# Low parts of the attention weights on GpSimd (POOL) in a two-block network

## The chip, the cores and the metric

The kernel runs on one core of a Trainium2 chip. The metric is the device time of one execution in microseconds. Engines are called by the names of the profile: PE is TensorE, PEld its weight load, DVE is VectorE, ACT is ScalarE, POOL is GpSimd, SP issues most transfers.

## The reference, cut to what matters

The reference is two transformer-like blocks on 256 tokens of width 1024, in float32. The part that the change touches is the token mixer of the first block:

```python
z_hy, q, k, v, gates = jnp.split(h @ w_in, SPLITS, axis=-1)
y_hy = hyena_branch(z_hy, conv_w, conv_b, filt, hy_bias) @ w_hy_out
q, k = apply_axial_rope(q, *rope), apply_axial_rope(k, *rope)
k = jnp.concatenate([k, ctx_kv[0]], axis=1)      # 256 more keys from the context
v = jnp.concatenate([v, ctx_kv[1]], axis=1)
...
p = jax.nn.softmax(s, axis=-1)
p = p[:, :, 0] - lam * p[:, :, 1]                # two softmax maps a head
```

Eight heads of 2 x 64 attend from 256 queries to 512 keys. Before the mixer stands a feed-forward network for tokens and context, after it a second one, then the second block with a recurrent branch, banded attention and sixteen experts.

## The kernel before

**Products in two parts.** TensorE multiplies rounded float32 numbers. To keep the precision, each operand is written as a high part, which is the rounded number, and a low part, which is the rest, and each product is three matmuls: high x high, high x low and low x high (`mm3`). `split` makes the two parts: ACT copies the source to the high part and DVE subtracts the high part from the source.

**Weights.** `weights` loads one block of 1024 x 256 weights (tile raw) through SP's queue and splits it in four pieces of 128x512, so each block costs four copies on ACT (whi) and four subtractions (wlo, line 140). There are three buffers for raw and two for each of the parts: the parts of a block can only be written when the matmuls of the block two before it are through.

**The attention groups.** `mixer` first ends the Hyena branch (`hyena_conv`, lines 734 to 736 multiply spectra on DVE) and then runs four groups of two heads. `kvq` makes one group's keys, queries and values from three weight blocks: the key block (512 columns of tokens and context), the query block, the value block. Keys and queries get a rotary embedding in `rope`: four DVE instructions that write tiles rb and ra (lines 765 to 768), then a split (kl, ql). Woven between these steps run the steps of `attend` for the group before: scores, exponentials on ACT, the scaling and sum of the two softmax maps on DVE (p, lines 958 to 961), transposes on TensorE (line 964), the split of the transposed map (pTl), the product with the values.

**Order.** The program text gives each instruction a priority. At the build a planner walks the whole program and writes a fixed order for each engine, taking the first in priority among the instructions that it believes to be ready. On the chip each engine then runs its list strictly in order and waits at semaphores. POOL has little in its list in this stage: the issue of the rotary table's transfer (line 821).

Of the kernel before, what the change touches and what calls it, by code (L numbers as in the profile page):

```python
# [20 lines left out]
T = 256  # L21
# [47 lines left out]
class Net:  # L69
# [52 lines left out]
        self.wp = self.pool(f"wp{n_raw}{n_split}", 1, side="left", es=self.wes)  # L122


    def weights(self, src, ring=False):

        nc = self.nc
        kt, cols = src.shape[1:]
        raw = self.raw_tile() if ring else self.wp.tile([128, kt, cols], F32, name="raw", tag="raw", bufs=self.n_raw)
        nc.sync.dma_start(out=raw, in_=src)  # L130
        hi = self.wp.tile([128, kt, cols], F32R, name="whi", tag="whi", bufs=self.n_split)
        lo = self.wp.tile([128, kt, cols], F32R, name="wlo", tag="wlo", bufs=self.n_split)
        n = max(1, min(kt, CUT // cols))
        for k in range(0, kt, n):
            self.split(raw[:, k:k + n], hi[:, k:k + n], lo[:, k:k + n])
        return hi, lo

    def split(self, src, hi, lo, eng=None):
# [11 lines left out]
        for _ in self.gemm_steps(*args, **kw):  # L150
            pass

    def gemm_steps(self, src, x, n, consume, c0=0, c1=None, steps=1, ring=False, whole=False):


        i = 0
        for c in range(c0, src.shape[0] if c1 is None else c1):
            hi, lo = self.weights(src[c], ring)
            kt, w = src.shape[2:]
            for m in range(w // 128):  # L160
                ps = self.mm([128, n])
                s = slice(m * 128, m * 128 + 128)
                for k in range(kt):
                    with self.tc.high_priority() if whole and k % (kt // steps) else ExitStack():
                        self.mm3(ps, (hi[:, k, s], lo[:, k, s]), (x[0][:, k, :], x[1][:, k, :]), k == 0, k == kt - 1)
                    if k < kt - 1 and (k + 1) % (kt // steps) == 0:
                        yield
                consume(i, ps)
                i += 1
                yield  # L170
# [290 lines left out]
    def first_ffn(self):  # L461
# [21 lines left out]
        with ExitStack() as es2:  # L483
# [13 lines left out]
            def weights(n):  # L497
# [3 lines left out]
                for i in range(2):  # L501
                    self.split(w[i][0][:, s], w[i][1][:, s], w[i][2][:, s])

            weights(0)
            diag = []
            for i in range(4):
# [16 lines left out]
            for f in range(KT + 1):  # L523
                if f < KT:
                    if f + 1 < KT:
                        raws.append(self.ada_load(f + 1, tmp))
                        if f % 2:
                            weights(f // 2 + 1)
                    row = self.ada_rows_of(raws[f], tmp)
                    ps = self.aux([128, 2 * T])  # L530
                    self.turned(ps, x, f, diag)
                if f:
                    products(f - 1, (0, 1))
                if f < KT:
                    a = self.ada_columns(f, row)
                    for i in range(2):
                        t = self.wk.tile([128, T], F32, name="nt", tag="nt", bufs=3)
                        nc.scalar.activation(out=t, in_=ps[:, cut[i]], func=AF.Identity, scale=a[:, i:i + 1],
                                             bias=self.mods[:, f, i:i + 1])
                        self.split(t, h[0][:, f, cut[i]], h[1][:, f, cut[i]])  # L540
                if f:
                    products(f - 1, (2, 3))
# [243 lines left out]
    def mixer(self):  # L786
        nc = self.nc
        w = self.A["w_in"]
        h = self.h
        hx = [x[:, :, 0:T] for x in h]  # L790
        with ExitStack() as es:
# [32 lines left out]
            values = lambda: [pa.tile([128, 4, 256], F32R, name=f"v{q}", tag=f"v{q}", bufs=2) for q in "hl"]  # L824

            def kvq(g, kk, qq, v):
                hi, lo = self.weights(w[16 + g])
                for m in range(2):
                    ps = self.mm([128, 2 * T])
                    s = slice(m * 128, m * 128 + 128)  # L830
                    for k in range(KT):
                        self.mm3(ps, (hi[:, k, s], lo[:, k, s]), (h[0][:, k, :], h[1][:, k, :]), k == 0, k == KT - 1)
                        if k == 3:
                            yield
                    t = [pa.tile([128, 2 * T], F32R, name=f"k{q}", tag=f"k{q}", bufs=3) for q in "hl"]
                    self.rope(pa, ps[:, 0:T], rope[:, 2:4, :], t[0][:, 0:T], t[1][:, 0:T])
                    self.split(ps[:, T:], t[0][:, T:], t[1][:, T:])
                    kk.append(t)
                    yield

                def q_done(m, ps):
                    t = [pa.tile([128, T], F32R, name=f"q{q}", tag=f"q{q}", bufs=3) for q in "hl"]
                    self.rope(pa, ps, rope[:, 0:2, :], t[0], t[1])
                    qq.append(t)

                yield from self.gemm_steps(w, hx, T, q_done, 12 + g, 13 + g)
                hi, lo = self.weights(w[20 + g])
                v += values()
                for tt in range(4):
                    ps = self.mm([128, 256])  # L850
                    s = slice(tt * 128, tt * 128 + 128)
                    for k in range(KT):
                        self.mm3(ps, (h[0][:, k, s], h[1][:, k, s]), (hi[:, k, :], lo[:, k, :]), k == 0, k == KT - 1)
                    self.split(ps, v[0][:, tt, :], v[1][:, tt, :])
                    yield

            side = iter(())
            for g in range(4):
                kk, qq, v = [], [], []
                self.weave(kvq(g, kk, qq, v), side)  # L860
                for _ in side:
                    pass
                side = self.attend(pa, qq, kk, v, g, o)
            gate = [x.bitcast(F32)[:, m, :] for x in values() for m in range(4)]
            for _ in range(2):
                for q in "hl":
                    x = pa.tile([128, 2 * T], F32, name="gda", tag=f"k{q}", bufs=3)
# [1109 lines left out]
```

## Time and profile before

| | |
|---|---|
| median of 3 runs | 1811.67 us (1810.1 to 1814.51) |
| the profiled execution | 1813.05 us |
| its span, first to last instruction | 1811.3 us |
| PE busy | 1687.9 us (93%) |
| DVE busy | 1009.7 us (56%) |
| ACT busy | 706.9 us (39%) |
| POOL busy | 19.9 us (1%) |
| mean granted clock of PE | 0.925 |

The busy times come from one profiled execution. PE's matmuls are pipelined and their ends are modelled, so its share is not the share of its peak. The attention groups take the stretch from about 505 to 700 us; the last quarter of the span is bound by the loads of the experts' weights.

### The profile page before, as it was taken

How to read it: one execution, taken by the hardware profiler on the slowest of the kernel's cores; microseconds unless marked ns; L12 is line 12 of the kernel's file. 1: busy time of each engine (PE TensorE's matmuls, PEld its weight loads, DVE VectorE, ACT ScalarE, POOL GpSimd, SP SyncE). 2: the span in 40 equal slices, each digit the busy share in tenths (PEclk: the TensorE clock that was granted, in tenths of full speed). 3: DMA queues.
4: the chain of work that ended last, by engine and by line, in shares of the span. 5: the costliest groups of instructions: out<-in, count | busy, mean ns of one | idle time of the engine just before them, and what ended most of it. 6: DMA issues, size and time to landing. Idle time of an engine off the chain costs nothing.

```text
span 1811.3 us, 33886 instructions
## 1 busy us (share of the span) xinstructions
PE 1687.9 (93%) x13847; PEld 1275.4 (70%) x13847; DVE 1009.7 (56%) x2502; ACT 706.9 (39%) x1515; POOL 19.9 (1%) x41
## 2 busy tenths in 40 slices
PE   8999999999999999999999999999999878787776
PEld 5788787788998889999999798888874222222222
DVE  3888776768987776676665768877740000000001
ACT  3532223657545568456444653456640000000001
POOL 0000000000000000000000000000010000000000
PEclk9999999999999999999999899999999676767678
DMA  8666673423432214546543331112799999999997
GB/s 330 217 219 231 220 260 112 133 82 121 155 108 94 91 70 140 187 148 248 187 163 117 115 123 61 49 61 76 298 400 400 409 408 409 409 408 409 408 409 303
DMA packets 97768, 397.85 MB, mean 220 GB/s; under 512 B 11227, under 2 KB 13708, under 8 KB 84044
## 3 DMA queue, kind: packets, MB, share of 16 engines
q1 hardware_dynamic: 91728, 386.97, 56.9%
q10 hardware_dynamic: 3724, 4.77, 0.8%
q0 software_dynamic: 2160, 3.94, 0.8%
q8 instruction: 109, 1.79, 0.4%
q14 instruction: 47, 0.39, 0.1%
HBM read 394.59 MB, written 1.05 MB: 218 GB/s over the span
## 4 chain that ended last, share of the span: by engine, by line
PE 68%; DMA 19%; DVE 8%; ACT 3%; issue 1%; DVEq 0%; ACTq 0%; SPq 0%
PE mm L145 13%; PE mm L147 12%; PE mm L146 12%; DMA raw<-exp_w_down 7%; DMA raw<-exp_w_gate 7%; PE mm L1572 4%; PE a L1383 4%; PE at L145 4%; PE at L146 4%; PE at L147 4%; PE a L1740 3%; DMA araw<-w_adat 2%; DMA raw<-exp_w_up 2%; DVE wlo L140 2%; DVE ajunk L310 2%
## 5 line engine op out<-in xcount | busy, mean ns | idle before, releaser
L139 ACT CAST whi<-raw 128x512 fp32r<-128x512 f32 x542 | 309.4, 618 | 260.6 <-PE mm L146 133.1
L140 DVE TENSOR_TENSOR wlo<-raw,whi 128x512 fp32r<-128x512 f32 x542 | 356.5, 686 | 97.8 <-ACT whi L139 93.5
L145 PE MATMUL mm<-hh,whi 128*128 128x256 f32 (+1 forms) x784 | 245.8, 315 | 0.5 <-DVE kl L140 0.5
L147 PE MATMUL mm<-hh,wlo 128*128 128x256 f32 (+1 forms) x784 | 244.9, 314 | 0.5 <-DVE wlo L140 0.2
L146 PE MATMUL mm<-hl,whi 128*128 128x256 f32 (+1 forms) x784 | 244.0, 312 | 0.0
L1707 DVE TENSOR_SCALAR scat<-iota,col 128x256 f32<-128x256 f32 x16 | 6.5, 412 | 275.0 <-PE a L1740 275.0
L145 PEld LDWEIGHTS mm<-hh,whi 128*128 128x128 f32 x784 | 147.2, 188 | 13.2 <-issue 3.5
L146 PEld LDWEIGHTS mm<-hl,whi 128*128 128x128 f32 x784 | 147.3, 188 | 9.9 <-issue 0.8
L147 PEld LDWEIGHTS mm<-hh,wlo 128*128 128x128 f32 x784 | 146.9, 188 | 10.0 <-DVE wlo L140 1.1
L1572 PE MATMUL mm<-raw,ehid 128*32 128x256 f32 x960 | 100.1, 513 | 40.6 <-DMA raw<-exp_w_down 40.2
L1744 ACT COPY ys<-mm 128x256 f32<-128x256 f32 (+1 forms) x20 | 7.2, 362 | 303.4 <-PE mm L1572 293.2
L310 DVE SCALAR_TENSOR_TENSOR ajunk<-araw,scr 128x512 bf16<-128x512 f32 x160 | 110.2, 689 | 27.6 <-DMA araw<-w_adat 25.5
L1572 PE MATMUL mm<-raw,xg 128*32 128x256 f32 x1024 | 103.1, 489 | 20.4 <-DMA raw<-exp_w_gate 20.4
L145 PE MATMUL at<-hh,whi 128*128 128x512 f32 (+1 forms) x352 | 118.7, 337 | 0.0
L147 PE MATMUL at<-hh,wlo 128*128 128x512 f32 (+1 forms) x352 | 118.4, 336 | 0.0
L146 PE MATMUL at<-hl,whi 128*128 128x512 f32 (+1 forms) x352 | 118.1, 336 | 0.0
L145 PE MATMUL mm<-whi,hidh 128*128 128x512 f32 x264 | 105.5, 400 | 1.1 <-ACT hidh L139 0.6
L147 PE MATMUL mm<-whi,hidl 128*128 128x512 f32 x264 | 104.8, 398 | 0.5 <-DVE hidl L140 0.4
L146 PE MATMUL mm<-wlo,hidh 128*128 128x512 f32 x264 | 104.8, 397 | 0.0
L1572 PEld LDWEIGHTS mm<-raw,ehid 128*32 128x32 f32 x960 | 23.7, 123 | 113.7 <-DMA raw<-exp_w_down 95.5
L1572 PE MATMUL a<-raw,xg 128*32 128x256 f32 x1024 | 83.9, 482 | 8.8 <-DMA raw<-exp_w_up 8.8
L145 PE MATMUL mm<-h2h,whi 128*128 128x256 f32 x296 | 89.7, 304 | 0.0
(630 smaller groups left out, 3391.9 us busy)
## 6 DMA issues: line engine op xcount, KB each, us to landing
raw<-exp_w_gate SPq DMA_DIRECT2D x128, 512.0 KB, 10.2
raw<-exp_w_up SPq DMA_DIRECT2D x128, 512.0 KB, 10.2
raw<-exp_w_down SPq DMA_DIRECT2D x120, 512.0 KB, 10.2
raw<-w_ff_in SPq DMA_DIRECT2D x42, 1024.0 KB, 4.8
raw<-w_in SPq DMA_DIRECT2D x32, 1024.0 KB, 4.7
araw<-w_adat SPq DMA_DIRECT2D x56, 512.0 KB, 4.7
raw<-w_ff_out SPq DMA_DIRECT2D x20, 1024.0 KB, 4.9
raw<-w_fill SPq DMA_DIRECT2D x22, 512.0 KB, 3.5
```

The source lines that it names most:

```text
L139: self.high = self.nc.scalar.copy(out=hi, in_=src)
L140: self.low = (eng or self.nc.vector).tensor_tensor(out=lo, in0=src, in1=hi.bitcast(F32), op=ALU.subtract)
L145: nc.tensor.matmul(out=ps, lhsT=w[0], rhs=x[0], start=first, stop=False)
L146: nc.tensor.matmul(out=ps, lhsT=w[0], rhs=x[1], start=False, stop=False)
L147: nc.tensor.matmul(out=ps, lhsT=w[1], rhs=x[0], start=False, stop=last)
L310: nc.vector.scalar_tensor_tensor(out=junk, in0=raw[:, s], scalar=1.0, in1=self.scr[v][:, s], op0=ALU.mult, op1=ALU.mult, accum_out=part[:, ...
L1383: self.nc.tensor.matmul(out=ps[r], lhsT=w[r], rhs=x[r], start=start, stop=stop)
L1572: nc.tensor.matmul(out=ps[q], lhsT=x(k), rhs=raw[:, j, :], start=(k == 0), stop=(k == KT - 1))
L1707: nc.vector.tensor_scalar(out=sc, in0=self.iota[:, 0:T], scalar1=col[:, 0, e:e + 1], scalar2=col[:, 1, e:e + 1], op0=ALU.is_equal, op1=ALU ...
L1740: nc.tensor.matmul(out=acc(tt, j), lhsT=sc[q, tt * 128:tt * 128 + 128], rhs=ys[q], start=False, stop=False)
L1744: nc.scalar.copy(out=ys, in_=ps)
```

## The change

The low parts of the twelve weight blocks that `kvq` loads (key, query and value of four groups) are subtracted by POOL in place of DVE. The operation and its operands are the same. All other blocks, and all other splits, stay on ACT and DVE. `split` had the argument for the engine already.

```diff
-    def weights(self, src, ring=False):
+    def weights(self, src, ring=False, low=None):
...
-            self.split(raw[:, k:k + n], hi[:, k:k + n], lo[:, k:k + n])
+            self.split(raw[:, k:k + n], hi[:, k:k + n], lo[:, k:k + n], low)
...
-    def gemm_steps(self, src, x, n, consume, c0=0, c1=None, steps=1, ring=False, whole=False):
+    def gemm_steps(self, src, x, n, consume, c0=0, c1=None, steps=1, ring=False, whole=False, low=None):
...
-            hi, lo = self.weights(src[c], ring)
+            hi, lo = self.weights(src[c], ring, low)
...
             def kvq(g, kk, qq, v):
-                hi, lo = self.weights(w[16 + g])
+                hi, lo = self.weights(w[16 + g], low=nc.gpsimd)
...
-                yield from self.gemm_steps(w, hx, T, q_done, 12 + g, 13 + g)
-                hi, lo = self.weights(w[20 + g])
+                yield from self.gemm_steps(w, hx, T, q_done, 12 + g, 13 + g, low=nc.gpsimd)
+                hi, lo = self.weights(w[20 + g], low=nc.gpsimd)
```

## Rows read from the trace of the kernel before

**Rows 1.** The page, chain that ended last: share of the span by engine

```profile
PE 68%; DMA 19%; DVE 8%; ACT 3%; issue 1%; DVEq 0%; ACTq 0%; SPq 0%
```

**Rows 2.** Busy time by stretch: start:end, length, engines, granted clock, DMA

```profile
505.00:528.00 23.00, 23.00 (x131) 19.52 (x130) 17.98 (x35) 7.60 (x14) 0.00 (x0) 1.00 0.26 92
...
585.00:626.00 41.00, 40.10 (x275) 34.37 (x274) 31.12 (x74) 23.02 (x51) 0.00 (x0) 1.00 0.22 78
```

**Rows 3.** Waits of PE, 505 to 668 us: total us, times, longest

```profile
PE at L964 <- DVE p L961: 2.3, 7, 0.5
PE mm L145 <- DVE kl L140: 0.5, 1, 0.5
```

**Rows 4.** Groups by line on DVE, 500.0 to 650.1 us: busy, mean ns | idle

```profile
L140 DVE TENSOR_TENSOR wlo<-raw,whi 128x512 fp32r<-128x512 f32 x48 | 32.0, 685 | 4.4 <-ACT whi L139 4.1
```

**Rows 5.** Groups by line on POOL, whole span

```profile
L140 POOL TENSOR_TENSOR hm<-hf,hm 128x256 fp32r<-128x256 f32 x8 | 6.0, 780 | 4.3 <-ACT hm L139 4.3
L1403 POOL COPY ip<-r 128x128 f32<-128x128 f32 x8 | 2.2, 297 | 645.3 <-DMA r<-r 512.8 <-PE a L1383 132.5
```

**Rows 6.** Timeline of DVE and POOL, 1336 to 1345 us: start, duration

```profile
1336.77 0.48 DVE L1625 TENSOR_SCALAR hf<-sx,rr 128x512 f32<-128x512 f32 x1
1336.86 0.98 POOL L140 TENSOR_TENSOR hm<-hf,hm 128x256 fp32r<-128x256 f32 x1 [4.34 <-ACT hm L139]
1337.16 0.96 DVE L1625 TENSOR_SCALAR hf<-sx,rr 128x512 f32<-128x512 f32 x1
...
1340.04 0.72 POOL L140 TENSOR_TENSOR hm<-hf,hm 128x256 fp32r<-128x256 f32 x1
1340.35 0.55 DVE L1647 TENSOR_TENSOR sel<-top,slotmask 16x128 f32<-16x128 f32 x1
...
1344.29 0.26 DVE L1647 TENSOR_TENSOR sel<-top,slotmask 16x128 f32<-16x128 f32 x1
```

**Rows 7.** Timeline of ACT and PE, first group's value weight

```profile
528.22 2.19 ACT L139 CAST whi<-raw 128x512 fp32r<-128x512 f32 x4 [6.67 <-PE mm L146]
...
534.46 0.28 PE L145 MATMUL mm<-whi,hh 128*128 128x256 f32 x1
```

**Rows 8.** Timeline of ACT and DVE, third group, 600 to 605 us

```profile
600.74 1.66 ACT L139 CAST whi<-raw 128x512 fp32r<-128x512 f32 x3 [0.24 <-PE mm L146]
...
601.89 0.42 DVE L767 TENSOR_TENSOR rb<-rb,rope 128x256 f32<-128x256 f32 x1
602.22 0.75 DVE L961 SCALAR_TENSOR_TENSOR p<-p,st 128x512 f32<-128x512 f32 x1
...
603.55 0.68 DVE L140 TENSOR_TENSOR wlo<-raw,whi 128x512 fp32r<-128x512 f32 x1
604.15 0.42 DVE L140 TENSOR_TENSOR kl<-ra,kh 128x256 fp32r<-128x256 f32 x1
604.49 0.68 DVE L140 TENSOR_TENSOR pTl<-at,pTh 128x512 fp32r<-128x512 f32 x1
```

**Rows 9.** Timeline of PE, the same stretch

```profile
603.11 0.30 PE L964 MATMUL at<-ident,p 128*128 128x128 f32 x1 [0.18 <-DVE p L961]
...
605.44 0.28 PE L146 MATMUL at<-pTl,vh 128*128 128x256 f32 x1
```

**Rows 10.** Timeline of ACT, DVE and PE, third group, 609 to 617 us

```profile
609.49 2.18 ACT L139 CAST whi<-raw 128x512 fp32r<-128x512 f32 x4 [1.42 <-PE mm L146]
...
615.75 0.74 DVE L961 SCALAR_TENSOR_TENSOR p<-p,st 128x512 f32<-128x512 f32 x1
...
616.54 0.33 PE L964 MATMUL at<-ident,p 128*128 128x128 f32 x1
```

**Rows 11.** Hyena products: groups on DVE, 500.0 to 650.1 us; timeline of PE

```profile
L736 DVE TENSOR_TENSOR prod<-prod 128x512 f32<-128x512 f32 x4 | 2.8, 690 | 0.1
...
511.97 0.38 PE L145 MATMUL at<-dft2h,yah 128*128 128x256 f32 x1
```

**Rows 12.** Waits of SP's queue, 1180 to 1340 us

```profile
SPq L130 <- DVE wlo L140: 78.1, 9, 14.4
```

## Prediction

> **What bounds the kernel now.** I read the page first. In the chain of work that ended last TensorE holds 68% and DMA 19% of the span, DVE 8% [rows 1]: most of the kernel is a queue of matmuls, and what DVE or POOL do counts only where TensorE waits for it. So the next view is the busy time by stretch [rows 2]. The changed weights are split between 500 and 650 us, and there TensorE is busy 23.00 of 23 us beside the last Hyena products and 40.10 of 41 us in a whole attention group, at a granted clock of 1.00, while DVE is busy 31.12 of 41 us and POOL not at all. The reader is to see that TensorE is full and DVE three quarters full: DVE's load is no bound as such. The list of TensorE's waits says what is left to win [rows 3]: 2.3 us for the scaled softmax rows p (seven times) and 0.5 us for a key's low part. Last I walked the timeline of one group, because the loss, if there is one, lies in the order of a few instructions on DVE.
>
> **What the change takes away.** Twelve weights (key, query and value in four groups) of four pieces make 48 low parts of 128x512, 32.0 us of DVE at 685 ns [rows 4]. TensorE does not run on DVE's load, so all that this can give back is the waits of [rows 3], some 3 us.
>
> **What it adds: 48 subtractions on POOL.** The same instruction runs on POOL in this kernel at half the size: 128x256, eight times, 780 ns mean [rows 5], 0.72 us when undisturbed [rows 6]. Twice that is 1.44 us, the upper bound for 128x512. For the lower bound I take the whole 297 ns of the 128x128 copy [rows 5] as a part that does not grow, and get 0.30 + 2 x (0.72 - 0.30) = 1.14 us. I take 1.25 us from one start to the next, since starts of neighbours lie closer than their durations. The Trainium skill, "GPSIMD Engine Reference", section "Performance versus the Vector engine", gives 4497 ns for 2048 elements; a quarter of it, 1.12 us, is an estimate from that page, and no run here shows it. By it the sum below would be some 2 us less.
>
> Is POOL in time? The tightest weight is the first group's value weight: its high parts start at 528.22 us and TensorE wants it from 534.46 us [rows 7]. The first high part is there at 528.84, so four low parts are there at 528.84 + 4 x 1.25 = 533.8. TensorE takes the last quarter only after 18 matmuls of 0.12 us, at 536.6, so POOL would be late only above (536.6 - 528.84) / 4 = 1.9 us a piece. Waiting for POOL itself costs nothing.
>
> **What it does to DVE.** [Rows 6] show DVE and POOL in each other's way. A DVE multiplication of 128x512 takes 0.48 us at 1336.77; the next one, issued while POOL subtracts from 1336.86 on, takes 0.96 us. The product sel of two SBUF tiles takes 0.26 us with POOL idle at 1344.29, and 0.55 us at 1340.35, where POOL's subtraction lasts from 1340.04 to 1340.76: it waited until POOL was nearly through. POOL's own first piece, begun during DVE's multiplication, took 0.98 in place of 0.72 us. So the two take turns by whole instructions. That they would not, or that larger DVE instructions escape, is the first rival. The Trainium skill says it more widely, "SBUF — State Buffer", section "SBUF: two separate sides": DVE with two SBUF inputs or in a two-port mode and GpSimd share one pair of ports under an exclusive lock, held for the whole instruction. The trace agrees with the 0.55 against 0.26 us; with the full 1.44 us as the time of the lock the sum below would be about 4 us more. This rule speaks against the change.
>
> Now the walk through one group, with 1.25 us a piece [rows 8, 9]. POOL's first piece can start when the first of the high parts is done, 600.74 + 0.62 = 601.4, and ends at 602.65. DVE's rotary product rb (two SBUF inputs) comes at 601.89, waits until 602.65 and ends at 602.98. POOL's second piece stands ready and takes 602.98 to 604.23. The scaled sum p, issued at 602.22 before, waits for it and ends at 604.98, 2.0 us later than before. TensorE's transposes of p wait 0.18 us for it already at 603.11 [rows 9], so they come 2.0 us later. It goes on: POOL 604.98 to 606.2, ra after it until 606.5, kl from the PSUM side until 606.8, POOL's fourth piece until 607.75, the second kl until 608.1, and pTl starts at 608.1 in place of 604.49. Its product stands at 605.44 on TensorE, so TensorE loses another 1.6 us. The one low part that DVE no longer does in this stretch (603.55) is counted in that. Sum: 3.6 us for the stretch, and three groups have it: 10.8 us.
>
> The next key weight falls on the same group's second half [rows 10]: high parts from 609.49 us, POOL from 610.1 to about 616. The products before p and p itself wait up to four times 1.25 us, while four low parts (4 x 0.65 = 2.6 us) leave DVE ahead of p; the rest, 5.0 - 2.6 = 2.4 us at most and nothing at least, I take at 1.2 us. TensorE takes p without a pause at 616.54, so it has no slack. Two groups: 2.4 us.
>
> In the first group there is no softmax yet. POOL's four pieces of the query weight (507.6 to about 513.7) fall among the Hyena products of two SBUF tiles, 0.69 us each [rows 11]. Two of them and one sum stand ahead of the matmul at 511.97 us; with the two low parts of DVE gone from there (1.3 us) and three waits of up to 1.25 us it comes 2.5 us later. The value weight then meets the two rotary steps of the keys, four products and two kl of two SBUF inputs. TensorE waits for the first kl already [rows 3]; at one wait of 1.25 us for each of POOL's four pieces less the 1.2 us of two low parts this is 3.8 us. Sum of the first group: 6.3 us, at least nothing where TensorE has other work.
>
> All together 10.8 + 2.4 + 6.3 = 19.5 us if every engine keeps its order. It will not: the order is made anew at the build with a lighter DVE, which can put p and pTl ahead of some waits. Lower bound for the effect of this: only the first wait of each of the three stretches is left, 3 x 2.0 = 6 us. Between 6 and 19.5 I take 15, nearer to the walk, since the rows of TensorE are full and each order leaves DVE's chain behind it. Later stages pass it on: the last loads wait for buffers that the split frees (78.1 us in nine waits [rows 12]), so the expert weights start later by as much.
>
> **The rivals.** First, DVE's waits are hidden, because the new order keeps the shared products out of POOL's time: then 0 to -3 us is left, 1811 us, no change. For it: DVE idles 10 of 41 us. Against it: TensorE has no slack at the chains. Second, the other side: DVE is relieved of 32 us, p and kl come sooner, and the new order also closes gaps beside the waits; the waits are worth 3 us, and it decides only if the order gains as much again, 1806 us. Against it: TensorE is busy 40.10 of 41 us. Third, POOL becomes the bound: if a piece with DVE's turns between takes more than 1.9 us, value weights come late; at 2.6 us that is 4 x 0.7 = 2.8 us in each of four groups, 11 us on top of the 15, 1838 us. Against it: 0.98 us was the longest at half size, 1.96 at double.
>
> **The numbers.** The profiled execution took 1813.05 us (span 1811.3), 1.4 us above the median of 1811.67; the 15 us are added to the median: 1827 us. Its own range is 1818 to 1832. Chances: the forecast 0.62, hidden 0.20, relief 0.05, POOL as bound 0.13. About 0.3% (5.4 us) is what this measurement can tell from no change. Slower holds the first and the last: 0.75; no change 0.20; faster 0.05. The range takes in most of the hidden case (1811) and reaches to the third rival: 1810 to 1838.
>
> **What the profile after would show.** The row of wlo on POOL, 48 times at 1.2 to 1.45 us; DVE's p, rb and ra with longer means than 0.75 and 0.42 us; the waits of TensorE for p, pTl and kl at over 10 us in place of 2.8; no wait of TensorE for a low part on POOL; and all stages after 700 us moved by the same amount. I am wrong if DVE's two-input products keep their durations beside POOL, or if they stretch and TensorE's waits stay near 3 us.

## The result, and the profile after

The changed kernel takes 1836.39 us (median of 4 runs, 1834.50 to 1840.87) against 1813.09 us before (median of 4, 1810.10 to 1816.13). The ratio is 1.0127 with a 95% interval of 1.0104 to 1.0150: slower by 23 us. The forecast was 1827 us, slower, in a range of 1810 to 1838. The profiled execution took 1834.5 us (span 1832.7).

Where does the time come in? Up to the mixer's Hyena products both traces run level. From 505 us on the one after falls behind step by step, is 23.4 us late at a matmul behind the third group's last scores (673.1 us before, 696.5 after), and some 20 to 23 us late from there to the end. So the loss is made in the stretch of the mixer in which the changed weights are split, and is passed on. The chain of work that ended last names the engines [rows 1]:

```profile
PE 65%; DMA 22%; DVE 9%; ACT 3%; issue 1%; DVEq 0%; SPq 0%; ACTq 0%
```

That says little: 23 of 1836 us are too few for shares. The useful view is the busy time of one stretch in which all kernels of this study do the same matmuls (two of them with some extra ones): from the first transposed Hyena input (uth on ACT) to the first matmul of the Hyena output weight. Columns as in [rows 2]. Before:

```profile
463.21:738.86 275.65, 271.45 (x1978) 245.40 (x1977) 209.02 (x456) 161.55 (x325) 0.53 (x1) 1.00 0.31 106
```

After:

```profile
462.53:762.26 299.73, 280.69 (x1978) 254.31 (x1976) 208.43 (x408) 161.17 (x325) 66.11 (x49) 0.97 0.29 97
```

The stretch is 24.1 us longer, and this splits in two. TensorE's idle time goes from 275.65 - 271.45 = 4.20 to 299.73 - 280.69 = 19.04 us: 14.8 us more. Its busy time, with the same 1978 matmuls, goes from 271.45 to 280.69: 9.2 us more, and the granted clock of the stretch is 0.97 in place of 1.00.

**The idle time.** The list of TensorE's waits, 505 to 692 us after, answers [rows 3]:

```profile
PE at L964 <- DVE p L961: 13.1, 8, 4.0
PE at L145 <- ACT yah L139: 3.0, 1, 3.0
PE at L145 <- ACT pTh L139: 1.6, 2, 0.8
PE aux L1211 <- DVE orms L979: 0.4, 2, 0.2
```

The waits for p grew from 2.3 to 13.1 us. The wait for a key's low part is gone, and no line names a low part of a weight: POOL is in time. Its row, same stretch (groups by line):

```profile
L140 POOL TENSOR_TENSOR wlo<-raw,whi 128x512 fp32r<-128x512 f32 x48 | 65.6, 1396 | 152.8 <-ACT whi L139 152.8
```

The groups by line on DVE, 462.53 to 762.26 us after:

```profile
L961 DVE SCALAR_TENSOR_TENSOR p<-p,st 128x512 f32<-128x512 f32 x16 | 14.0, 873 | 0.3
L768 DVE TENSOR_TENSOR ra<-ra,rb 128x256 f32<-128x256 f32 x16 | 12.9, 806 | 0.2
L767 DVE TENSOR_TENSOR rb<-rb,rope 128x256 f32<-128x256 f32 x16 | 11.8, 739 | 0.0
...
L960 DVE TENSOR_SCALAR p<-p,st 128x512 f32<-128x512 f32 x16 | 8.4, 527 | 0.0
...
L140 DVE TENSOR_TENSOR kl<-ra,kh 128x256 fp32r<-128x256 f32 x8 | 6.8, 847 | 0.9 <-ACT kh L139 0.3
L140 DVE TENSOR_TENSOR vl<-mm,vh 128x256 fp32r<-128x256 f32 x16 | 6.6, 420 | 9.7 <-ACT vh L139 9.7
...
L140 DVE TENSOR_TENSOR kl<-mm,kh 128x256 fp32r<-128x256 f32 x8 | 3.3, 415 | 0.0
```

The same groups before, 463.21 to 738.86 us:

```profile
L961 DVE SCALAR_TENSOR_TENSOR p<-p,st 128x512 f32<-128x512 f32 x16 | 12.0, 748 | 0.3
...
L768 DVE TENSOR_TENSOR ra<-ra,rb 128x256 f32<-128x256 f32 x16 | 6.7, 419 | 0.0
L767 DVE TENSOR_TENSOR rb<-rb,rope 128x256 f32<-128x256 f32 x16 | 6.7, 416 | 0.0
```

The reader is to compare the two kinds of kl: the one that subtracts two SBUF tiles (kl from ra) takes 847 ns, the one with a PSUM input (kl from mm) 415, and so does vl. The instructions of DVE that got longer read two SBUF tiles, with one exception, the scaling of p on line 960, which reads one tile and a column (480 ns before, 527 after). DVE's busy time is about that of before (208.43 and 209.02 us) although 48 instructions left it.

One wait in full: the timeline of DVE at the second group's value weight. POOL's four pieces run from 564.01 to 569.36.

```profile
563.65 0.42 DVE L767 TENSOR_TENSOR rb<-rb,rope 128x256 f32<-128x256 f32 x1
563.98 0.16 DVE L958 RECIPROCAL st<-st 128x2 f32<-128x2 f32 x1
564.10 1.49 DVE L768 TENSOR_TENSOR ra<-ra,rb 128x256 f32<-128x256 f32 x1
565.52 1.24 DVE L959 TENSOR_TENSOR st<-st,nlam 128x1 f32<-128x1 f32 x1
566.68 0.41 DVE L140 TENSOR_TENSOR kl<-mm,kh 128x256 fp32r<-128x256 f32 x1
567.01 1.23 DVE L960 TENSOR_SCALAR p<-p,st 128x512 f32<-128x512 f32 x1
568.17 1.48 DVE L140 TENSOR_TENSOR kl<-ra,kh 128x256 fp32r<-128x256 f32 x1
569.57 0.74 DVE L961 SCALAR_TENSOR_TENSOR p<-p,st 128x512 f32<-128x512 f32 x1
```

Four instructions stand for most of a piece of POOL each, with one that has a PSUM input (kl from mm, 0.41) between them: ra 1.49 in place of 0.42, the factor of one column 1.24 in place of 0.16, the scaling of p 1.23 in place of 0.48, kl 1.48 in place of 0.42. Then POOL is done, and p itself takes its normal 0.74. On TensorE, whose transposes wait for it:

```profile
570.46 0.63 PE L964 MATMUL at<-ident,p 128*128 128x128 f32 x4 [4.00 <-DVE p L961]
```

The third group answers [rows 8, 9]. DVE:

```profile
611.75 1.18 DVE L767 TENSOR_TENSOR rb<-rb,rope 128x256 f32<-128x256 f32 x1
612.85 1.75 DVE L961 SCALAR_TENSOR_TENSOR p<-p,st 128x512 f32<-128x512 f32 x1
614.52 1.49 DVE L768 TENSOR_TENSOR ra<-ra,rb 128x256 f32<-128x256 f32 x1
...
616.49 0.94 DVE L140 TENSOR_TENSOR kl<-ra,kh 128x256 fp32r<-128x256 f32 x1
617.35 0.68 DVE L140 TENSOR_TENSOR pTl<-at,pTh 128x512 fp32r<-128x512 f32 x1
```

TensorE:

```profile
614.75 0.63 PE L964 MATMUL at<-ident,p 128*128 128x128 f32 x4 [1.95 <-DVE p L961]
...
616.99 0.58 PE L145 MATMUL at<-pTh,vh 128*128 128x256 f32 x1 [0.79 <-ACT pTh L139]
```

The second of these waits comes by way of ACT, which makes the key's high part kh from the late ra before it makes pTh:

```profile
616.05 0.41 ACT L139 CAST kh<-ra 128x256 fp32r<-128x256 f32 x1 [2.95 <-DVE ra L768]
616.36 0.58 ACT L139 CAST pTh<-at 128x512 fp32r<-128x512 f32 x1
```

**The longer matmuls.** Busy time by stretch, just behind the 4.00 us wait:

```profile
570.50:571.80 1.30, 1.30 (x11) 1.13 (x11) 1.27 (x5) 0.59 (x1) 0.00 (x0) 1.00 0.48 88
571.80:575.20 3.40, 3.40 (x16) 3.40 (x17) 0.97 (x2) 0.41 (x1) 0.00 (x0) 0.50 0.59 248
575.20:578.00 2.80, 2.75 (x19) 2.07 (x18) 1.67 (x4) 2.12 (x5) 1.05 (x1) 1.00 0.00 0
```

From 571.8 us TensorE has work without a break but is granted 0.50, its 1.2 GHz level, and gets 16 matmuls done in 3.4 us, 0.21 us each against 0.12 just before. The records of the clock show this at five places, 20.5 us in all: from 513.8, 571.8, 616.2 (6.8 us), 633.2 and 667.4 us, each at the end of a wait of 1.95 us or more or within 1.5 us behind it, but for the last, which follows two waits of 1.95 and 0.79 us close together. Before, the clock was 1.00 in the whole stretch. Not all of the 9.2 us need be the clock: the kernel with quarter pieces (below) is 2.0 us more busy than before with no lower clock at all.

### The profile page after: what moved, and what is told of

Read it like the earlier page. It is cut to its first block, busy times and chain, and to the rows that moved or that the text cites. A ratio compares the mean times of both kernels' runs of the same rounds, so it can differ in the third digit from the quotient of the medians.

```text
span 1832.7 us, 33891 instructions
## 1 busy us (share of the span) xinstructions
PE 1675.5 (91%) x13847; PEld 1267.0 (69%) x13847; DVE 1009.4 (55%) x2454; ACT 706.3 (39%) x1515; POOL 86.0 (5%) x89
## 4 chain that ended last, share of the span: by engine, by line
PE 65%; DMA 22%; DVE 9%; ACT 3%; issue 1%; DVEq 0%; SPq 0%; ACTq 0%
PE mm L145 13%; PE mm L147 13%; PE mm L146 13%; DMA raw<-exp_w_down 7%; DMA raw<-exp_w_up 6%; DMA raw<-exp_w_gate 6%; PE a L1383 4%; PE at L145 4%; PE at L146 4%; PE at L147 3%; DMA araw<-w_adat 2%; PE mm L1572 2%; DVE ajunk L310 2%; DVE wlo L140 1%; PE a L1740 1%
## 5 line engine op out<-in xcount | busy, mean ns | idle before, releaser
L140 DVE TENSOR_TENSOR wlo<-raw,whi 128x512 fp32r<-128x512 f32 x494 | 324.6, 686 | 91.2 <-ACT whi L139 88.1
L147 PEld LDWEIGHTS mm<-hh,wlo 128*128 128x128 f32 x784 | 148.4, 190 | 10.2 <-DVE wlo L140 1.2
L1572 PE MATMUL mm<-raw,xg 128*32 128x256 f32 x1024 | 99.4, 483 | 8.4 <-DMA raw<-exp_w_gate 8.1
L1718 DVE TENSOR_TENSOR ea<-ea,a 128x256 f32<-128x256 f32 x16 | 6.7, 421 | 159.5 <-PE a L1572 159.5
## 6 DMA issues: line engine op xcount, KB each, us to landing
raw<-exp_w_gate SPq DMA_DIRECT2D x128, 512.0 KB, 10.2
raw<-exp_w_up SPq DMA_DIRECT2D x128, 512.0 KB, 10.2
raw<-exp_w_down SPq DMA_DIRECT2D x120, 512.0 KB, 10.2
```

Source lines behind the costliest of these rows:

```text
L140: self.low = (eng or self.nc.vector).tensor_tensor(out=lo, in0=src, in1=hi.bitcast(F32), op=ALU.subtract)
L147: nc.tensor.matmul(out=ps, lhsT=w[1], rhs=x[0], start=False, stop=last)
L1572: nc.tensor.matmul(out=ps[q], lhsT=x(k), rhs=raw[:, j, :], start=(k == 0), stop=(k == KT - 1))
L1718: nc.vector.tensor_tensor(out=a, in0=a, in1=u, op=ALU.mult)
```

## The experiments

Three theories. **A**, that of the prediction with the clock added: DVE's instructions on two SBUF tiles and POOL's take turns by whole instructions, TensorE waits for the chain behind them, and long waits let its clock fall. **B**: the lighter DVE list gets another order at the build, and that order costs the time. **C**: POOL's low parts are late (four take 5.5 us in place of 2.7), and what needs them or their buffers is late. Edits are shown against the kernel after. Every kernel was timed beside the one before, whose median was 1810.6 to 1812.0 us in these series. Rows are of the stretch defined above, from one profiled execution of each kernel. The growth of this stretch comes within 2 us of the growth of the median in all kernels but two: with p in PSUM it is 14.1 us against 18.8, in the first fill 28.3 against 24.5.

### Adding alone, removing alone

```diff
-            self.split(raw[:, k:k + n], hi[:, k:k + n], lo[:, k:k + n], low)
+            self.split(raw[:, k:k + n], hi[:, k:k + n], lo[:, k:k + n]); low and low.tensor_tensor(out=self.spare, ...)
```

> DVE keeps all 48 low parts, and POOL does the same 48 subtractions once more into a tile that nobody reads. Theory A (DVE instructions with two SBUF inputs and POOL's take turns; the waits let TensorE's clock fall): nothing is taken off DVE and POOL is in the way as often, so the loss is at least that of the change, 20 to 32 us: 1833 to 1845 us, TensorE's idle time of 510 to 697 us at 15 us or more in place of 3.25, and low granted clocks behind the long waits. Theory B (the lighter DVE list and the new order that follows from it cost the time): DVE's list is as long as before, so no loss, 1813 us. Theory C (POOL's low part is late, 5.5 us a weight in place of 2.7, and what waits for it or for its buffers is late): nobody reads POOL's tile, so 1813 to 1816 us.

Measured: 1849.25 us, ratio 1.0214 (1.0196 to 1.0233), 38 us slower, more than the change itself.

```profile
461.63:776.40 314.77, 287.16 (x1978) 259.12 (x1977) 250.89 (x456) 161.78 (x325) 73.52 (x49) 0.94 0.26 93
```

Idle time is 27.61 us, 23.4 more than before, busy time 15.7 us more, with 37.5 us at the lower clock. B in its form (a lighter list) and C fall as sole causes: DVE has all its 456 instructions, and nobody reads what POOL writes. DVE's order still differs from that before in some twenty places, so what a new order costs is left to the next kernel. The size lies above my 20 to 32 us: DVE's own low parts wait too (902 ns mean in place of 685), and TensorE now waits for them:

```profile
PE mm L146 <- DVE wlo L140: 2.0, 2, 1.3
```

The opposite:

```diff
-        lo = self.wp.tile(..., name="wlo", ...)
+        lo = self.wp.tile(..., name="wlo", ...) if not low else hi
-            self.split(raw[:, k:k + n], hi[:, k:k + n], lo[:, k:k + n], low)
+            self.nc.scalar.copy(out=hi[:, k:k + n], in_=raw[:, k:k + n]) if low else self.split(...)
```

> The 48 low parts are not computed by any engine: TensorE takes the high part of these twelve weights in place of the low part. DVE's order is that of the kernel after, and POOL is empty in this stretch. It measures what the relief of DVE and the new order are worth by themselves. Theory A: the waits of TensorE that DVE's load can give back are the 3 to 4 us of the kernel before, so 0 to -3 us, 1808 to 1812 us, with DVE's rb, ra and p at 0.42 and 0.75 us. Theory B (the new order costs the time): 1836 us, with the waits of the kernel after.

Measured: 1810.32 us, ratio 1.0003 (0.9991 to 1.0015).

```profile
461.43:737.51 276.08, 271.99 (x1978) 245.94 (x1977) 182.96 (x408) 160.78 (x325) 0.53 (x1) 1.00 0.30 106
```

DVE is 26 us less busy than before, in exactly the order that it has after, and TensorE's idle time is 4.09 us, as before. So the new order of DVE costs nothing (B is out), and the relief of DVE is worth nothing: the change could not have gained.

### One kind of weight at a time

The argument low is left in one of the three places (value: the weight w[20 + g]; query: w[12 + g]; key: w[16 + g]).

> Only the value weights' 16 low parts on POOL. Theory A reads its share off the waits that stand beside the value weights in the trace after: 4.00 us (at 570.46), 1.95 and 0.79 (614.75, 616.99), 1.95 and 0.79 (664.95, 667.19), 9.5 us in all, and 13.6 of the 20.4 us at the lower clock, which at 8.6 us lost in 20.4 are 5.7 us more: 15 us, some 1828 us (1824 to 1831). Theory B (order): a third of the change's low parts and so about a third of its loss, 1821 us. Theory C (lateness): the value weights have the tightest time, so nearly all of the 23 us, 1834 us, with TensorE waiting for wlo.

> Only the query weights' 16 low parts on POOL. Theory A: beside the query weights the trace after has one wait, 2.96 us for the Hyena product's high part at 513.96, and 3.4 us at the lower clock (1.4 us lost): 4.4 us, 1817.5 us (1813 to 1820). Theory B: a third of the loss, 1821 us. Theory C: 1813 us, since TensorE never waits for a query weight.

> Only the key weights' 16 low parts on POOL. Theory A: the waits beside key weights in the trace after are 1.04, 0.54, 2.48 and 0.64 us, 4.7 us, and 3.4 us at the lower clock (1.4 us lost): 6 us, 1819 us (1815 to 1822). The three parts add up to 25 us by this reading, against 23 us measured together. Theory B: a third of the loss, 1821 us, and the sum of the three need not fit. Theory C: 1813 us.

Measured: value 1824.18 us, ratio 1.0072 (1.0052 to 1.0092), query 1814.94 us, 1.0024 (1.0012 to 1.0037), key 1816.71 us, 1.0038 (1.0026 to 1.0050). Value:

```profile
465.54:755.61 290.07, 275.48 (x1977) 248.91 (x1976) 213.14 (x440) 161.01 (x325) 22.89 (x17) 0.98 0.29 101
```

Query:

```profile
463.75:743.00 279.25, 272.65 (x1978) 246.75 (x1976) 202.84 (x440) 161.33 (x325) 21.26 (x17) 0.99 0.30 104
```

Key:

```profile
459.17:739.56 280.39, 272.02 (x1978) 245.65 (x1976) 210.80 (x440) 161.71 (x325) 23.35 (x17) 1.00 0.29 104
```

Sixteen POOL instructions each, and 13, 4 and 6 us lost: the number of instructions is not what counts. Each lies within A's range, all three in its lower half. For the value weights alone B's 1821 us lies in the interval too; for the query and the key weights it does not.

In the value kernel the waits that A had read off the trace are there (3.87 us, then 1.96 and 0.80, 1.96 and 0.79), and two more beside the first group's value weight, 1.24 us for kl and 0.56 for ra. The lower clock came less often than in the kernel after: 10.2, 3.4 and 0 us in the profiles, in place of 13.6, 3.4 and 3.4. The profile of the key kernel is from the quickest of its twelve executions. The three losses add up to 22.7 us, against 23.3 together, but this fit is in part luck: the extra idle time of the three adds up to 17.0 us against 14.8, the extra busy time to 5.8 against 9.2.

Then the query weights without those of the first group, `low=nc.gpsimd if g else None`:

> Only the query weights of groups 1 to 3 on POOL, 12 low parts: the ones beside which the trace after shows no wait of TensorE. Theory A: POOL works where DVE has no two-input instruction that TensorE waits for, so no loss, and a relief of 8.2 us of DVE that gives back at most the waits: 1809 to 1813 us. Theory B (order) or any theory in which each POOL piece costs the same: a quarter of the loss, 1818 us.

Measured: 1810.65 us, ratio 1.0008 (0.9995 to 1.0020).

```profile
460.74:736.00 275.26, 271.35 (x1977) 245.37 (x1976) 201.35 (x444) 161.41 (x325) 15.64 (x13) 1.00 0.30 106
```

Twelve low parts on POOL cost nothing, since they delay nothing on DVE: none of its instructions is longer than before, and p, ra and rb keep 747, 417 and 415 ns. They gain nothing either.

### The length of a turn

POOL's piece is cut, the high part on ACT stays 128x512. Halves (`weights` calls this helper in place of `split` for the twelve blocks):

```diff
+    def two(self, src, hi, lo, eng):
+        self.nc.scalar.copy(out=hi, in_=src)
+        for j in range(2): eng.tensor_tensor(out=lo[:, j:j + 1], in0=src[:, j:j + 1], in1=hi[:, j:j + 1].bitcast(F32), op=ALU.subtract)
```

> The change, but POOL does each 128x512 low part as two pieces of 128x256; the high parts and the order of the instructions on TensorE and DVE are the same as in the kernel after. Theory A (turns by whole instructions, and the clock falls behind long waits): an instruction of DVE waits for 0.72 us at most in place of 1.25, so the extra idle time of TensorE is about half of the 14.8 us, 6 to 9 us, few waits stay above 2 us, and the lower clock takes 2 to 4 us in place of 9: 1820 to 1825 us. Theory B (new order): the order is the one that is said to cost the time, so 1836 us. Theory C (POOL's low parts are late): POOL needs as long or longer for a weight, 8 x 0.72 = 5.8 us, so 1836 us or more.

Measured: 1826.45 us, ratio 1.0090 (1.0072 to 1.0108).

```profile
461.28:750.28 289.00, 275.15 (x1978) 248.64 (x1977) 200.96 (x408) 161.00 (x325) 78.48 (x97) 0.99 0.29 101
```

Quarters, by the same helper with four pieces of 128 columns:

> The change, but POOL does each low part as four pieces of 128x128; order on TensorE and DVE as in the kernel after. Extra idle time of TensorE against the length of a turn: 14.8 us at 128x512 (1.40 us mean), 9.7 at 128x256 (0.85). Theory A: a turn of 128x128 is shorter again, 0.4 to 0.55 us, so 5 to 8 us of extra idle time and 0 to 3 us for the clock: 1817 to 1823 us, although POOL's total time grows, 16 x 0.45 = 7.2 us or more for a weight. Rival: the total time that POOL is busy decides, or the number of turns: 1826 us, as with halves, or more.

Measured: 1817.01 us, ratio 1.0045 (1.0027 to 1.0063).

```profile
462.58:744.33 281.75, 273.47 (x1978) 245.66 (x1976) 192.44 (x408) 160.96 (x325) 97.63 (x193) 1.00 0.30 104
```

With an unchanged order on TensorE and DVE, POOL's time in the stretch rises from 66 to 78 and 97 us, and the loss falls from 23 to 14 and 6 us by the medians (23, 16 and 8 by the ratios); the extra idle time from 14.8 to 9.7 and 4.1 us. That is against C, for which a busier POOL is a later POOL. A's bounds were not quite met: for halves the time came out 1.5 us above its range and the extra idle time 9.7 us against 6 to 9, for quarters 4.1 us against 5 to 8. Where a half piece stands in the way it costs 0.5 to 0.6 us (ra 947 ns at the longest in place of 419), but there are twice as many.

A copy in place of the subtraction, in the kernel with the spare tile, `low.tensor_copy(out=self.spare, in_=hi[:, k:k + n].bitcast(F32))`:

> As the spare subtractions (DVE keeps all its low parts), but POOL only copies the high part into the tile that nobody reads: one SBUF input in place of two. Theory A in its wide form (any POOL instruction on SBUF takes a turn): a loss in proportion to the copy's duration, which lies between 0.30 us (the 128x128 copy as it stands) and 1.19 us (four times that), 10 to 35 us of the 38 measured with two inputs, 1821 to 1846 us. Theory A in its narrow form (only a POOL instruction with two SBUF inputs gets in the way): 1811 to 1814 us, and DVE's rb and ra stay at 0.42 us.

Measured: 1816.62 us, ratio 1.0029 (1.0015 to 1.0042).

```profile
461.99:742.57 280.58, 272.23 (x1977) 245.55 (x1976) 220.97 (x456) 160.80 (x325) 40.08 (x49) 1.00 0.30 104
```

Neither bound held. The narrow form is wrong: DVE's ra rises to 831 ns and p to 1093 at the longest, so a POOL instruction with one SBUF input takes turns too. But a turn costs DVE 0.41 us and not 0.8 (the copy's mean duration beside DVE), and the loss is 5 us, less than the 10 that I gave as the least.

### An operand in PSUM

```diff
-                    t = pa.tile([128, 2 * T], F32, name="p", tag=f"p{mp}", bufs=2 - mp)
+                    t = ps if mp else pa.tile([128, 2 * T], F32, name="p", tag=f"p{mp}", bufs=2 - mp)
```

> The change, but the second map of exponentials stays in its PSUM bank, so DVE's scaled sum p has one SBUF and one PSUM input in place of two SBUF inputs. Theory A: kl and vl, which have a PSUM input, kept 0.42 us beside POOL in the trace after, so p does too: its mean falls from 0.95 back to about 0.75 us, and the waits of TensorE for p from 13.1 to 5 to 9 us, 1826 to 1832 us. Rival (p is late because rb and ra ahead of it are, or the PSUM banks held longer make new waits): p's own duration falls, but TensorE's idle time stays within 3 us of 18.9: 1833 to 1838 us.

Measured: 1830.80 us, ratio 1.0109 (1.0092 to 1.0126). Groups on DVE:

```profile
L961 DVE SCALAR_TENSOR_TENSOR p<-at,st,p 128x512 f32<-128x512 f32 x16 | 12.0, 747 | 0.3
L767 DVE TENSOR_TENSOR rb<-rb,rope 128x256 f32<-128x256 f32 x16 | 11.8, 741 | 0.0
```

Waits of TensorE in the stretch:

```profile
PE at L964 <- DVE p L961: 9.8, 10, 2.8
```

The product p is back at its time of before, 747 ns, beside the same POOL work, while rb, left on two SBUF inputs, is not. TensorE waits 9.8 us for p in place of 14.0 in the same stretch; what is left fits rb (741 ns), ra and the factors ahead of p, which still meet POOL. Its idle time is 13.8 us, 5.2 less than after: the time lies in A's range, but the waits for p above its 9 us, so the rival's cause is there too. This profile is from the quickest of the four executions (1823.68 us); where the others spend 7 us more is not shown.

### The clock

Extra matmuls ahead of the four groups of transposes that wait longest:

```diff
+                [self.tc.keep_in_program_order(nc.tensor.matmul(out=ps, lhsT=self.idle[:, 0:128], rhs=self.idle, ...)) for _ in range(FILLS.get((g, m, qt), 0))]
                 for i in range(4):
                     nc.tensor.transpose(out=ps[:, i, :], in_=p[0]...)
```

> The change, with 36 extra matmuls of 128x512 (bf16, 0.25 us each, result overwritten) ahead of the four groups of transposes of p that wait longest in the trace after (15, 6, 9 and 6 of them for 4.00, 1.95, 2.48 and 1.95 us). They take the place of idle time and bring nothing. Theory A with the clock as a term of its own: TensorE no longer idles for 2 us there, the granted clock stays at 1.00 behind three or four of the five waits, and 6 to 8 of the 9.2 us of longer matmuls come back: 1828 to 1831 us. Rival (the waits alone make the loss, and the clock falls for another reason or costs nothing): p comes as late as before, so 1836 us, or more where the extra matmuls delay it.

Measured: 1836.45 us, ratio 1.0138 (1.0121 to 1.0155). This one told little about the clock. The timeline of TensorE:

```profile
564.85 3.41 PE L962 MATMUL at<-idle 128*128 128x512 bf16 x14
...
572.38 0.90 PE L964 MATMUL at<-ident,p 128*128 128x128 f32 x3 [3.88 <-DVE p L961]
```

The build put the extra matmuls where real ones had stood and moved those behind the transposes, so that the wait stayed at 3.88 us. The next kernel ties them to the wait: a small matmul ahead of them reads the softmax factor that DVE makes just before p.

```diff
+                nc.tensor.matmul(out=ps[:, 0, 0:1], lhsT=self.ident, rhs=st[:, 3:4], start=True, stop=True)
```

> As the fill before, but the extra matmuls (11, 5, 7 and 5 of 0.25 us) stand behind a small matmul that reads the softmax factor of the same rows, so that they run inside the waits and not ahead of them. Some 1.5 us of real matmuls are moved behind the transposes at each of the four places, which costs up to 4 to 6 us. Theory A with the clock as a term of its own: the waits are cut into pieces of about 1 to 2 us with work between, at least half of the 20.5 us at the lower clock are gone in the mixer's stretch, and 4 to 9 us of longer matmuls come back: 1830 to 1836 us. Rival (the lower clock does not come from these waits): 20 us at the lower clock as before, and 1838 to 1843 us.

Measured: 1834.80 us, ratio 1.0140 (1.0114 to 1.0166).

```profile
563.82 0.35 PE L962 MATMUL at<-st,ident 128*128 128x1 f32 x2 [2.04 <-DVE st L959]
564.25 2.32 PE L962 MATMUL at<-idle 128*128 128x512 bf16 x10
567.29 0.33 PE L964 MATMUL at<-ident,p 128*128 128x128 f32 x1 [0.72 <-DVE p L961]
```

Its stretch:

```profile
459.16:759.77 300.61, 282.03 (x2009) 251.29 (x2012) 208.94 (x408) 161.20 (x325) 66.64 (x50) 0.99 0.28 97
```

The wait is cut in two, and the lower clock is granted for 6.8 us in place of 20.5, gone behind three of the four places. What is left of it, two times 3.4 us, stands where a long wait was left: behind the 2.96 us for the Hyena product, which was not filled, and at the third place, where 2.34 us of waiting come ahead of the extra matmuls:

```profile
627.36 0.47 PE L962 MATMUL at<-st,ident 128*128 128x1 f32 x2 [2.34 <-DVE st L959]
```

Without the rows of the extra matmuls the 282.03 us of busy time are 274.3, so that the kernel's own take 2.8 us more than before in place of 9.2. So filling the waits brings back two thirds of this term. But the extra matmuls take 7.8 us, and the idle time is still 18.6 us, since real matmuls moved behind the transposes: no gain.

No version here beats the kernel before.

## Why the prediction was right, and where not

**TensorE is full, and DVE's relief is worth 3 us at most**: right; without the low parts on any engine the time is that of before within 0.15%. This closes the second rival (relief, given 0.05).

**POOL takes 1.25 us and is in time**: right. Undisturbed its pieces last 1.26 to 1.30 us, the mean beside DVE is 1.40, the longest 1.74, and TensorE waits for none. The third rival (above 1.9 us) did not come.

**DVE and POOL take turns by whole instructions**: right, by the rows of DVE, by the longer loss when only POOL's work is added, and by the loss that follows the length of a turn. The instruction with a PSUM operand keeps its time. This also answers what the paragraph on DVE called the first rival, that larger instructions escape: p of 128x512 does not (873 ns against 748 before). The Trainium skill, "SBUF — State Buffer", section "SBUF: two separate sides", says that a DVE instruction with two SBUF inputs or in a two-port mode and a GpSimd instruction exclude each other for a whole instruction; these runs agree (p 873 against 747 ns with its operand moved to PSUM, beside the same POOL work). But DVE lost 1.07 us at a turn (ra 1.49 against 0.42, issued 0.09 us behind POOL's first piece) where POOL's instruction lasted 1.26 or more, so the full duration of POOL's row would be too high a price.

**The walk through a group**: the places were right, and the first step of the path; the sizes were not all right. The third group's transposes were to come 2.0 us later; TensorE's wait is 1.95, 1.8 more than at the same place before. The second step was wrong: pTl on DVE was to hold up its product by another 1.6 us, but TensorE waits for no pTl. It loses 0.79 us to the high part pTh on ACT, which stands behind the late kh. For the second group the walk had not seen that the factor st and the scaling of p meet POOL too: 4.0 us, 3.7 more than before. Together the three groups give 8.9 us more waiting in place of 10.8. The key weights cost more than the 2.4 us taken: waits of 1.04 and 0.54, and of 2.48 and 0.64 us, stand beside them, 3.8 us more than at the same places before.

**The first group** was over-sized: 6.3 us forecast. The Hyena product waits 2.96 us (2.5 forecast), but the value weight's 3.8 us did not come, and the 0.5 us that TensorE had waited for kl is gone: 2.4 us. With another order such a wait does come: in the value kernel TensorE waits 1.24 and 0.56 us there.

**The discount from 19.5 to 15**: the extra idle time is 14.8 us, so the amount fits, but that is luck. I expected the new order to put p ahead of some waits; nothing in these runs shows that. The terms came out as 8.9, 3.8 and 2.4 us in place of 10.8, 2.4 and 6.3, and another wait of 0.2 us is gone: most of what is missing is the first group's value weight, and the key weights take some of it back.

**The term that was missing**: the sum was made at a granted clock of 1.00, which I had read in the first paragraph, and held it constant while adding waits. The waits made it fall, and 9.2 us of longer matmuls came on top of 14.8 us of waits: 24 us in place of 15. That is why 1836 us lies above the likeliest case's own range (1818 to 1832). It lies inside the stated 1810 to 1838 only because that range was stretched to the third rival, which did not come; that part is luck. That the lower clock follows the waits is shown by the late fill, and by the other kernels: none of the five whose longest wait in the stretch is 1.31 us or less (before, no low parts, queries 1 to 3, quarters, copy) has it, and of the rest all but the key kernel have. Which waits let it fall is not settled: 2.50 us in the key kernel and 2.83 us with p in PSUM were not followed by it, 1.24 and 0.56 us close together in the value kernel were, and the pairs of 1.95 and 0.79 us were followed by it in the kernel after and not in the value kernel.

**The first rival (hidden)** came true for a quarter of the change, the query weights of groups 1 to 3, which cost nothing by themselves, and beside the first group's value weight no wait stands either. The rest is not hidden.

**Passed on one to one**: right; 23.4 us at 697 us, 21.4 by the spans. SP's nine waits for buffers that the split frees take 78.0 us, as before.

## What to carry to other kernels

Before work is moved from DVE to POOL, list the DVE instructions on two SBUF tiles, and the scalings of one, that TensorE waits for, and place POOL's pieces where none of them runs; where that can't be, cut POOL's pieces short or give the DVE instruction an operand in PSUM, which made the loss here smaller and did not remove it. Moved work is no relief when the engine that it leaves waits as long as the work took: look for the wait inside the duration of the others. When waits are added ahead of matmuls, reckon the granted clock behind them as a term of its own, and read it as busy time that grows with the same number of matmuls.

## What was not expected of the hardware

- The size of a DVE instruction did not matter for its wait: the product of two columns of 128x1 took 1.24 us beside POOL in place of 0.16.
- The scaling of p by a column (one SBUF tile and a scalar column) waited too, 1.23 in place of 0.48 us, though the walk had counted two SBUF tiles only. The prediction's own [rows 6] held the sign, a scaling of 128x512 at 0.96 in place of 0.48 us.
- A one-input copy of 128x512 on POOL cost DVE 0.41 us a turn, the two-input subtraction of the same tile 1.07 us.
- TensorE was granted 0.50 while it was fully busy, 1.3 us after a wait of 4.00 us had ended, and 1.00 again at 575.2 us.
